# Cosine-similarity attention on one core: one score chunk of pair 24 exponentiated on VectorE, a shorter ring of cast V, a longer ring of exponentials, and new orders of work

## The chip, the core and the metric

The kernel runs on one core of one Trainium2 chip. The five engines that the profile names are TensorE (PE, with its weight loads as PEld), VectorE (DVE), ScalarE (ACT), GpSimd (POOL) and SyncE (SP), which here only issues transfers. The metric is the device time of the kernel in microseconds (us). Three runs of the kernel before gave 191.53, 191.48 and 190.59 us; the median is 191.48 us.

## The reference

Q, K and V have 8 batches of 12 heads, each 512 by 64, in float32, and tau is 0.1.

```python
Q_norm = Q / (np.linalg.norm(Q, axis=-1, keepdims=True) + 1e-10)
K_norm = K / (np.linalg.norm(K, axis=-1, keepdims=True) + 1e-10)
scores = np.einsum('bhqd,bhkd->bhqk', Q_norm, K_norm) / tau
weights = np.exp(scores - np.max(scores, axis=-1, keepdims=True))
weights = weights / (np.sum(weights, axis=-1, keepdims=True) + 1e-10)
return np.einsum('bhqk,bhkd->bhqd', weights, V)
```

Because the rows are normalised, a score lies between -10 and 10, and the kernel leaves the subtraction of the maximum out: a common factor of a row falls out when the row is divided by its sum.

## The kernel before, in words

The 96 heads are worked on as 48 pairs. All steps of a pair `s` are named, and a table (`ORDER`) lists, for each engine by itself, in which order that engine runs them. Nothing else decides the order: every engine runs its list from front to back, and a step that needs a result of another engine waits for that engine's semaphore, with everything behind it on the same list.

The steps of a pair are these.

- `LD.s.0`, `LD.s.1`, `LV.s` (SP): load Q, K and V of the pair, 256 KB each. `ST.s` stores the result.
- `SQ.s` (POOL): squares of Q and K in bf16 (line 250). `SSQ.s` (PE): eight matmuls with the identity that fold the squares into partial sums (line 268). `RED.s` (DVE): the sums of squares (line 276).
- `NEW.g.0` to `NEW.g.7` (DVE): inverse square roots by Newton steps, for a group `g` of one or two pairs, in the bank `nps` of PSUM (lines 397 to 409). The first three pairs take a logarithm (`LN`) and an exponential (`EX`, line 286) on ACT instead.
- `SCL.s.0` (DVE) and `SCL.s.1` (mostly POOL): Q and K times their inverse norms, to bf16 (line 296).
- `TR.s` (PE): sixteen transposes into PSUM (line 498). `EVA.s` (DVE): the copy of these to SBUF, the tile `qt` (line 504).
- `SCO.s.c` for four chunks `c` (PE): two matmuls of 512 columns, the scores of 128 keys against 512 queries for both heads (line 526). There are two buffers of scores, so `SCO` of a chunk has to wait until `EXP` two chunks earlier has read its buffer.
- `EXP.s.c` (ACT): the exponential of 1024 scores a partition, to bf16 in the tile `et` (line 542).
- `PV.s.h.t` (PE): eight groups of four matmuls of 65 columns, the exponentials times V with a column of ones (line 570). V is cast to bf16 by `VC.s` (POOL, line 547) into the ring `vb`.
- `RCP.s` and `NRM.s` (DVE): one over the row sums, and the product that makes the output (lines 584 and 586).

The chunks of all pairs form one sequence. PE works some pairs ahead of the products: while the scores of pair `s` are made, the products of pair `s-2` run between them. Below, a *slot* is what PE does from one `SCO` to the next.

The program can already put a chunk on DVE (the function `split`, steps `SCD` on PE and `EXD` on DVE), but the table `SPLIT` that names the chunks is empty, so that this code is not run. `SCD` makes the scores on top of a constant ("level") in PSUM, so that the bits of the float are already a linear guess of the exponential's bf16 bits; four steps `EXD.0` to `EXD.3` correct the guess by a cubic and write the 16 bits into `et`.

Of the kernel before, what the change touches and what calls it, by code (L numbers as in the profile page):

```python
# [28 lines left out]
class Program:  # L29
# [95 lines left out]
def bass_cosine_similarity_attention_kernel(  # L125
# [16 lines left out]
    R_QK, R_V, R_SQ, R_QN, R_QT, R_ET, R_O = 18, 6, 6, 5, 5, 3, 8  # L142
# [8 lines left out]
    vb = sb("vb", [128, R_QK, NT, 2, DIM + 1], bf16)  # L151
# [11 lines left out]
    level = sb("level", [128, 128 + SEQ], bf16)  # L163
    wd = [sb(f"wd{i}", [128, SEQ], f32) for i in range(2)]
# [51 lines left out]
    def scored(s):  # L216

        if s < 0:
            return []
        last = [("SCO", s, NT - 1) if s else ("SCO", 0, 1, NT - 1)]  # L220
        return last + [("SCD", s, h) for h in range(2) if s in SPLIT]

# [204 lines left out]
    def pair(s):  # L427
# [24 lines left out]
        if 0 < s < LOGS:  # L452
# [9 lines left out]
            for w, dst in ((0, rq), (1, r)):  # L462
                exps(s, (w,), dst, xl[s][:, w], ("LN", s), gain, free)
            scaled(s, 0, "dve", rq, [("EX", s, 0), ("EX", s, 1)])
            for j in range(2) if s == 1 else ():
                scaled(1, 1, eng, r, [("EX", 1, w) for w in range(2)], (j,), slice(2 * j, 2 * j + 2))
            if s > 1:
                scaled(s, 1, eng, r, [("EX", s, w) for w in range(2)])
        elif s:
# [5 lines left out]
            else:  # L475
                free = [("EX", LOGS - 1, w) for w in range(2)]
# [39 lines left out]
        for c in range(NT) if s else ():  # L516
# [23 lines left out]
            else:  # L540
# [5 lines left out]
        P.add(("VC", s), "pool", [("LV", s), key("PV", s - R_QK, 1, NT - 1), "vone"],  # L546
              lambda e: e.tensor_scalar(  # L547
                  out=vb[:, iq, :, :, 0:DIM].rearrange("p c h d -> p h c d"),
# [5 lines left out]
        for c in range(NT) if s in CHUNKED else ():  # L554
            def pv(e, c=c):
                for h in range(2):
                    for t in range(NT):
                        last = e.matmul(  # L558
                            out=o_ps[:, h, 65 * t : 65 * t + 65],
                            lhsT=et[iet][:, c, h, 128 * t : 128 * t + 128], rhs=vb[:, iq, c, h, :],  # L560
# [3 lines left out]
            P.add(("PV", s, c), "pe", [("EXP", s, c), ("VC", s), ("PV", s, c - 1) if c else None], pv,  # L564
                  take=[] if c else ["o0", "o1"], until=("NRM", s))
        for h in range(2) if s not in CHUNKED else ():
            for t in range(NT):
                def pv(e, h=h, t=t):
                    for c in range(NT):
                        last = e.matmul(  # L570
                            out=o_ps[:, h, 65 * t : 65 * t + 65],
                            lhsT=et[iet][:, c, h, 128 * t : 128 * t + 128], rhs=vb[:, iq, c, h, :],
# [5 lines left out]
                      [("EXP", s, NT - 1) if s else ("EXP", 0, 1, 1), ("VC", s), before,  # L578
                       *([("EXD", s, h, 3)] if s in SPLIT else []),
# [13 lines left out]
    def split(s, c, ready, iqt, iet):  # L593

        for h in range(2):
            hs = slice(64 * h, 64 * h + 64)

            def scd(e, hs=hs):
# [259 lines left out]
```

## Time and profile before

| | |
|---|---|
| median of three runs | 191.48 us (190.59 to 191.53) |
| span of the profiled execution, first to last instruction | 189.4 us |
| mean granted TensorE clock | 0.996 |
| ACT busy | 181.7 us, 96% |
| PE busy, modelled | 174.1 us, 92% |
| POOL busy | 160.7 us, 85% |
| DVE busy | 148.1 us, 78% |
| DMA | 50.8 MB, mean 268 GB/s |

The profile gives the span of its execution and no other time of it. The median of the runs is 2.1 us above that span. That is what lies around the first and the last instruction, and the difference between executions. A row of the page's groups reads: line, engine, operation, output from inputs, shapes, count, then the busy time, the mean length of one in ns, and the idle time just before. A row of the timeline begins with the start and the length in us; rows of the same kind in a run are merged with their count. Instructions of one engine may overlap at their ends, so the length of one is longer than the step from one start to the next.

### The profile page before, as it was taken

To read this page: it belongs to the slowest core of one execution; us is meant where nothing else is said; L and a number is where in the kernel's file an instruction comes from. 1 tells how busy PE (TensorE), PEld (TensorE's weight loads), DVE (VectorE), ACT (ScalarE), POOL (GpSimd) and SP (SyncE) were. 2 spreads that over 40 slices of the span, in tenths; PEclk is the share of its full clock that TensorE was granted. 3 is DMA by queue.
4 is the path that set the end of the run, shared out by engine and by line. 5 is a ranking of instruction groups with operands and counts; after the bars stand their busy time and mean duration, and the time that the engine had idled before them with its cause. 6 is when DMAs were issued, how large, how long until landed. Compare 5 with 4: busy or idle time off the path is not lost.

```text
span 189.4 us, 7341 instructions
## 1 busy us (share of the span) xinstructions
PE 174.1 (92%) x3078; PEld 110.7 (58%) x3078; DVE 148.1 (78%) x453; ACT 181.7 (96%) x210; POOL 160.7 (85%) x147
## 2 busy tenths in 40 slices
PE   7989998999999998999999999989989999987893
PEld 5446664665665665666555666556656666654552
DVE  1999987879877886898876968969888787787624
ACT  5699999999999999999999999999999999999993
POOL 1799999999999999999999999999997599562500
PEclk9999999999999999999999999999999999999998
DMA  6999999999469999999999959899959500754435
GB/s 169 338 352 349 350 350 349 350 376 383 151 197 356 291 345 315 269 376 323 359 361 378 271 167 336 257 332 345 328 160 313 168 12 9 211 177 140 141 107 173
DMA packets 52448, 50.80 MB, mean 268 GB/s; under 512 B 3136, under 2 KB 52416, under 8 KB 52416
## 3 DMA queue, kind: packets, MB, share of 16 engines
q1 hardware_dynamic: 51984, 50.02, 82.3%
q8 instruction: 24, 0.39, 0.9%
q10 hardware_dynamic: 432, 0.33, 0.6%
q14 instruction: 8, 0.07, 0.1%
HBM read 37.75 MB, written 12.58 MB: 266 GB/s over the span
## 4 chain that ended last, share of the span: by engine, by line
ACT 82%; DVE 7%; PE 7%; DMA 1%; issue 1%
ACT et L542 80%; PE scps L526 2%; DMA qk<-in_Q_dram 1%; DVE qn L296 1%; PE bps L570 1%; DVE ob L586 1%; DVE qt L504 1%; ACT et L371 1%; PE bps L339 1%; PE bps L558 1%; DVE nps L276 1%; PE bps L268 1%; DVE ob L643 1%; PE bps L498 0%; DVE xs L324 0%
## 5 line engine op out<-in xcount | busy, mean ns | idle before, releaser
L542 ACT ACTIVATE et<-scps 128x1024 bf16<-128x1024 f32 x184 | 169.1, 1128 | 0.5 <-PE scps L526 0.4
L250 POOL TENSOR_TENSOR sq<-qk 128x1024 bf16<-128x1024 f32 (+2 forms) x48 | 87.9, 1848 | 5.1 <-DMA qk<-in_Q_dram 4.9
L526 PE MATMUL scps<-qt 64*128 64x512 bf16 x376 | 74.4, 385 | 8.4 <-ACT et L542 6.1
L570 PEld LDWEIGHTS bps<-vb,et 128*128 128x128 bf16 x1472 | 51.4, 98 | 24.1 <-issue 18.0
L570 PE MATMUL bps<-vb,et 128*128 128x65 bf16 x1472 | 65.1, 194 | 0.2
L296 POOL TENSOR_TENSOR qn<-qk,rk 128x512 bf16<-128x512 f32 x44 | 45.8, 1051 | 11.8 <-DVE rk L405 11.7
L504 DVE COPY qt<-bps 128x1024 bf16<-128x1024 bf16 x46 | 31.8, 691 | 10.1 <-PE bps L498 9.4
L296 DVE TENSOR_TENSOR qn<-qk,nps 128x512 bf16<-128x512 f32 (+1 forms) x51 | 33.9, 671 | 0.8 <-ACT nps L286 0.2
L586 DVE TENSOR_TENSOR ob<-bps,rd 128x512 f32<-128x512 f32 x47 | 32.5, 691 | 1.2
L526 PEld LDWEIGHTS scps<-qt 64*128 64x128 bf16 x376 | 18.2, 93 | 25.3 <-ACT et L542 13.4
L547 POOL TENSOR_SCALAR vb<-vf 128x512 bf16<-128x512 f32 x48 | 29.9, 634 | 0.0
L268 PE MATMUL bps<-sq,ident 128*128 128x128 bf16 x376 | 29.1, 220 | 0.0
L268 PEld LDWEIGHTS bps<-sq,ident 128*128 128x128 bf16 x376 | 21.2, 98 | 9.4 <-issue 6.3
L584 DVE RECIPROCAL rd<-bps 128x8 f32<-128x8 f32 x47 | 9.7, 207 | 17.7 <-PE bps L570 14.3
L498 PE MATMUL bps<-ident,qn 64*128 64x64 bf16 x736 | 18.8, 191 | 2.4 <-DVE ob L586 0.4
L498 PEld LDWEIGHTS bps<-ident,qn 64*128 64x128 bf16 x736 | 14.2, 95 | 9.8 <-DVE nps L276 4.0
L276 DVE TENSOR_REDUCE nps<-bps 128x16 f32<-128x128 f32 x45 | 13.4, 297 | 1.8 <-PE bps L268 1.8
L397 DVE TENSOR_TENSOR nps<-nps,ys 128x32 f32<-128x32 f32 (+1 forms) x48 | 9.2, 193 | 0.9
L401 DVE SCALAR_TENSOR_TENSOR nps<-nps,ys 128x32 f32<-128x32 f32 (+1 forms) x48 | 9.1, 191 | 0.8
L237 PE MATMUL scps<-warm_in 128*128 128x256 bf16 x22 | 4.8, 402 | 1.1 <-DVE warm_in L232 1.1
L409 DVE TENSOR_SCALAR ys<-nps 128x32 int32<-128x32 int32 (+1 forms) x24 | 4.4, 183 | 0.5
L405 DVE SCALAR_TENSOR_TENSOR nps<-nps,ys 128x16 f32<-128x16 f32 (+1 forms) x25 | 4.3, 175 | 0.3
(44 smaller groups left out, 47.4 us busy)
## 6 DMA issues: line engine op xcount, KB each, us to landing
vf<-in_V_dram SPq DMA_DIRECT2D x48, 256.0 KB, 5.4
qk<-in_Q_dram SPq DMA_DIRECT2D x47, 256.0 KB, 5.9
qk<-in_K_dram SPq DMA_DIRECT2D x47, 256.0 KB, 5.7
out_dram<-ob SPq DMA_DIRECT2D x47, 256.0 KB, 4.4
qk<-in_Q_dram SPq DMA_DIRECT2D x2, 128.0 KB, 2.7
qk<-in_K_dram ACTq DMA_DIRECT2D x2, 128.0 KB, 2.9
out_dram<-ob SPq DMA_DIRECT2D x1, 128.0 KB, 2.2
out_dram<-ob SPq DMA_DIRECT2D x1, 64.0 KB, 1.9
```

The lines of the kernel that those rows point to most:

```text
L250: emit = lambda e: e.tensor_tensor(out=b, in0=a, in1=a, op=ALU.mult)
L268: last = e.matmul(out=ps[:, 0:128], lhsT=ident[:, :], rhs=sq[s % R_SQ][:, :, 8 * k : 8 * k + 8], start=(k == 0), stop=(k == 7))
L276: lambda e: e.tensor_reduce(out=dst(None), in_=ps[:, 0:128].rearrange("p (w g e) -> p w g e", w=2, e=8), axis=AX.X, op=ALU.add))
L296: lambda e: e.tensor_tensor(out=o, in0=x, in1=r, op=ALU.mult))
L498: last = e.transpose(t_ps[:, k, b, :], qn[s % R_QN][ks, b // NT, b % NT].rearrange("p h d -> p (h d)"), ident[ks, ks])
L504: lambda e, lo=lo, hi=hi: e.tensor_copy(out=qt[iqt][:, :].rearrange("p w t (k x) -> p k (w t) x", k=2)[:, :, lo:hi], in_=t_ps[:, :, lo:hi]))
L526: last = e.matmul(out=sc_ps[:, 2 * b + k, :], lhsT=qt[iqt][64 * h : 64 * h + 64, 1, n, :], rhs=qt[iqt][64 * h : 64 * h + 64, 0, :, :], sta ...
L542: lambda e, c=c, b=b: e.activation(out=et[iet][:, c, :, :], in_=sc_ps[:, 2 * b : 2 * b + 2, :], func=ACT.Exp, scale=scale, bias=bias))
L547: lambda e: e.tensor_scalar(out=vb[:, iq, :, :, 0:DIM].rearrange("p c h d -> p h c d"), in0=vf[iv][:, :, :].rearrange("p h (c d) -> p h c ...
L570: last = e.matmul(out=o_ps[:, h, 65 * t : 65 * t + 65], lhsT=et[iet][:, c, h, 128 * t : 128 * t + 128], rhs=vb[:, iq, c, h, :], start=(c = ...
L584: lambda e: e.reciprocal(out=rd[io][:, :], in_=grid[:, :, :, DIM]))
L586: lambda e: e.tensor_tensor(out=ob[io][:, :], in0=grid[:, :, :, 0:DIM], in1=rd[io][:, :].unsqueeze(3).to_broadcast([128, 2, NT, DIM]), op= ...
```

## The change

Six things are edited.

1. `SPLIT = {24: 1}`: chunk 1 of pair 24 leaves ACT and PE's sequence of scores (`EXP.24.1` and `SCO.24.1` are gone). DVE makes its exponentials. The three other chunks of pair 24 get a constant bias so that both ways have the same scale; the factor falls out with the row sum.
2. `split` is rewritten: the chunk is cut into four parts (head `h`, half `j` of the queries) of 256 columns, and their scores go to the upper half of the bank `nps` instead of a bank of their own. Each part has one `SCD` on PE (two matmuls of 256 columns) and four `EXD` on DVE. A part's `SCD` waits for the last step of the part before, and, by the new lines in `schedule`, for the last step on DVE's list before its first `EXD` that touches the bank `nps` (a `RED`, `NEW`, `SCL` or `EXD`), since PE writes into that bank.
3. The ring of exponentials `et` has four buffers instead of three (`R_ET`), so that `EXP.s` waits for the products of pair `s-4` instead of `s-3`. The ring of cast V, until now as long as that of Q and K (18), has nine (`R_VB`), so `VC.s` waits for the products of pair `s-9`.
4. `SCL.12.1` and `SCL.18.1` go from POOL to DVE, each with one short `NEW` step more.
5. In the first pairs, where DVE scales both Q and K, the two `EX` of 8 columns on ACT become one of 16 (pairs 1 and 2).
6. The lists of all engines are written anew. SP's too: but for two loads that trade places the first 32 transfers keep their sequence, later some loads and stores trade places.

```diff
+        last = None
+        for o in order["dve"]:
+            if o.key[0] == "EXD" and o.key[-1] == 0:
+                self.ops[("SCD", *o.key[1:-1])].needs.append(last)
+            if o.key[0] in ("RED", "NEW", "SCL", "EXD"):
+                last = o.key
...
-    R_QK, R_V, R_SQ, R_QN, R_QT, R_ET, R_O = 18, 6, 6, 5, 5, 3, 8
+    R_QK, R_V, R_SQ, R_QN, R_QT, R_ET, R_O, R_VB = 18, 6, 6, 5, 5, 4, 8, 9
...
-    y_u = x_ps[:, :].bitcast(u16).rearrange("p (x two) -> p x two", two=2)[:, :, 0]
+    y_ps = n_ps[:, 256:512]
+    y_u = y_ps.bitcast(u16).rearrange("p (x two) -> p x two", two=2)[:, :, 0]
...
-            for w, dst in ((0, rq), (1, r)):
-                exps(s, (w,), dst, xl[s][:, w], ("LN", s), gain, free)
+            both = eng == "dve"
+            for w, dst in ((0, spare[:, 16 * s - 8 : 16 * s + 8]),) if both else ((0, rq), (1, r)):
+                exps(s, (w,), dst, xl[s][:, :, :].rearrange("p w x -> p (w x)") if both else xl[s][:, w], ("LN", s), gain, free)
...
-        P.add(("VC", s), "pool", [("LV", s), key("PV", s - R_QK, 1, NT - 1), "vone"],
+        P.add(("VC", s), "pool", [("LV", s), key("PV", s - R_VB, 1, NT - 1), "vone"],
...
+            for j in range(2):
+                hs, qs = slice(64 * h, 64 * h + 64), slice(256 * j, 256 * j + 256)
+                def scd(e, hs=hs, j=j):
+                    e.matmul(out=y_ps, lhsT=level[hs, 0:128], rhs=level[hs, 128:384], start=True, stop=False)
+                    return e.matmul(
+                        out=y_ps, lhsT=qt[iqt][hs, 1, c, :], rhs=qt[iqt][hs, 0, 2 * j : 2 * j + 2, :], start=False, stop=True)
+                P.add(("SCD", s, h, j), "pe", ready + ["level"] + exd[-1:], scd)
+                w = wd[len(exd) % 2][:, :]
+                steps = [
+                    lambda e, w=w: e.tensor_scalar(
+                        out=w, in0=y_u, scalar1=1.0, scalar2=-65536.0, op0=ALU.mult, op1=ALU.add),
+                    lambda e, w=w: e.tensor_tensor(out=w, in0=y_u, in1=w, op=ALU.mult),
+                    lambda e, w=w: e.scalar_tensor_tensor(
+                        out=w, in0=y_u, scalar=65536.0 * CUBIC[1], in1=w, op0=ALU.add, op1=ALU.mult),
+                    lambda e, w=w, h=h, qs=qs: e.scalar_tensor_tensor(
+                        out=et[iet][:, c, h, qs].bitcast(u16), in0=w, scalar=128 * CUBIC[0] / 65536.0**3, in1=y_ps,
+                        op0=ALU.mult, op1=ALU.add)]
...
-ON = {'SQ.0.0.1': 'pool', 'SCL.2.1': 'dve', 'SCL.3.1': 'dve', 'LD.1.1': 'sp', 'SCL.1.1': 'dve'}
-SPLIT = {}
+ON = {'SQ.0.0.1': 'pool', 'SCL.2.1': 'dve', 'SCL.3.1': 'dve', 'LD.1.1': 'sp', 'SCL.1.1': 'dve', 'SCL.12.1': 'dve', 'SCL.18.1': 'dve'}
+SPLIT = {24: 1}
...
-        PV.22.0.0 PV.22.0.1 TR.25 SCO.24.1 PV.22.0.2 PV.22.0.3 SCO.24.2 PV.22.1.0 PV.22.1.1 PV.22.1.2 PV.22.1.3
+        SCO.24.0 PV.22.0.1 PV.22.0.2 PV.22.0.3 SCD.24.1.0 SCO.24.2 SSQ.29 SCO.24.3 PV.22.1.0 PV.22.1.1 PV.22.1.2
```

What the new lists do is seen at three places. The first is PE's list at the scores of pair 24. In these rows `scps<-qt` is an `SCO` (two matmuls a chunk), `bps<-vb,et` are products (four matmuls a group), `bps<-ident,qn` is a `TR`, `bps<-sq,ident` an `SSQ`, `nps<-level` with `nps<-qt` an `SCD`. Before, from `TR.25` to `SSQ.29`:

```order
L498 MATMUL bps<-ident,qn 128x64 x16
L526 MATMUL scps<-qt 128x512 x2
L570 MATMUL bps<-vb,et 128x65 x8
L526 MATMUL scps<-qt 128x512 x2
L570 MATMUL bps<-vb,et 128x65 x16
L526 MATMUL scps<-qt 128x512 x2
L268 MATMUL bps<-sq,ident 128x128 x8
```

With the change, from `SCD.24.0.1` to `SSQ.29`:

```order
L610 MATMUL nps<-level 128x256
L611 MATMUL nps<-qt 128x256
L535 MATMUL scps<-qt 128x512 x2
L580 MATMUL bps<-vb,et 128x65 x4
L507 MATMUL bps<-ident,qn 128x64 x16
L535 MATMUL scps<-qt 128x512 x2
L580 MATMUL bps<-vb,et 128x65 x12
L610 MATMUL nps<-level 128x256
L611 MATMUL nps<-qt 128x256
L535 MATMUL scps<-qt 128x512 x2
L275 MATMUL bps<-sq,ident 128x128 x8
```

One `SCO` is gone (24.1), and two `SCD` stand directly ahead of `SCO.23.3` and `SCO.24.2`. The second place is DVE's list at the same time. Here `rd<-bps` is an `RCP`, `ob<-bps` an `NRM`, `nps<-bps` a `RED`, `qt<-bps` an `EVA`, `wd<-nps` and `et<-wd,nps` are `EXD`, the short ones with `ys` are `NEW`. Before, from `EVA.24` to `EVA.25`:

```order
L504 COPY qt<-bps 128x2x8x64
L401 SCALAR_TENSOR_TENSOR nps<-nps,ys 128x32
L584 RECIPROCAL rd<-bps 128x8
L586 TENSOR_TENSOR ob<-bps,rd 128x512
L276 TENSOR_REDUCE nps<-bps 128x2x8
L405 SCALAR_TENSOR_TENSOR ys<-nps,ys 128x32
L397 TENSOR_TENSOR nps<-nps,ys 128x32
L401 SCALAR_TENSOR_TENSOR nps<-nps,ys 128x32
L405 SCALAR_TENSOR_TENSOR nps<-nps,ys 128x16
L405 SCALAR_TENSOR_TENSOR rk<-nps,ys 128x16
L504 COPY qt<-bps 128x2x8x64
```

With the change, from the end of part 0 to `EVA.25` (the seven rows ahead of these are `EVA.24`, the first three `EXD` of part 0, two `NEW` and `RCP.21`):

```order
L622 SCALAR_TENSOR_TENSOR et<-wd,nps 128x256
L596 TENSOR_TENSOR ob<-bps,rd 128x512
L617 TENSOR_SCALAR wd<-nps 128x256
L283 TENSOR_REDUCE nps<-bps 128x2x8
L619 TENSOR_TENSOR wd<-nps,wd 128x256
L408 SCALAR_TENSOR_TENSOR nps<-nps,ys 128x32
L620 SCALAR_TENSOR_TENSOR wd<-nps,wd 128x256
L412 SCALAR_TENSOR_TENSOR nps<-nps,ys 128x16
L622 SCALAR_TENSOR_TENSOR et<-wd,nps 128x256
L513 COPY qt<-bps 128x2x8x64
```

Eight `EXD` now stand between the two `EVA`, and the other eight between `EVA.25` and `EVA.27`, always with another step between two of them but for the last pair. The third place is PE's list at the scores of pair 20. Before, from `SCO.20.1` to `SCO.20.3`:

```order
L526 MATMUL scps<-qt 128x512 x2
L498 MATMUL bps<-ident,qn 128x64 x16
L570 MATMUL bps<-vb,et 128x65 x8
L526 MATMUL scps<-qt 128x512 x2
L570 MATMUL bps<-vb,et 128x65 x16
L526 MATMUL scps<-qt 128x512 x2
```

With the change, from `SCO.20.1` to `TR.22`; the row of four is `SCO.20.2` and `SCO.20.3`:

```order
L535 MATMUL scps<-qt 128x512 x2
L580 MATMUL bps<-vb,et 128x65 x16
L275 MATMUL bps<-sq,ident 128x128 x8
L535 MATMUL scps<-qt 128x512 x4
L507 MATMUL bps<-ident,qn 128x64 x16
```

The slot of `SCO.20.1` now holds four groups of products and an `SSQ`; before, an `SSQ` behind four groups stood in the slots of `SCO.3.0` and `SCO.40.2` alone.

More of the change, by code (lines that the diff above doesn't have):

```diff
@@ L220, in scored @@
         last = [("SCO", s, NT - 1) if s else ("SCO", 0, 1, NT - 1)]
-        return last + [("SCD", s, h) for h in range(2) if s in SPLIT]
+        return last + [("SCD", s, h, j) for h in range(2) for j in range(2) if s in SPLIT]
     P.add("one", "pool", [], lambda e: e.memset(ones[:, :], 1.0))
@@ L595, in split @@
         for h in range(2):
-            hs = slice(64 * h, 64 * h + 64)
-            def scd(e, hs=hs):
-                e.matmul(out=x_ps[:, :], lhsT=level[hs, 0:128], rhs=level[hs, 128 : 128 + SEQ], start=True, stop=False)
-                return e.matmul(out=x_ps[:, :], lhsT=qt[iqt][hs, 1, c, :], rhs=qt[iqt][hs, 0, :, :], start=False, stop=True)
-            P.add(("SCD", s, h), "pe", ready + ["level"], scd, take=["x"], until=("EXD", s, h, 3))
-            w, done = wd[len(exd) % 2], exd[-2:-1]
```

328 lines of the change are left out of this document (165 added, 163 removed).

## The prediction

> **What bounds the kernel now.** I read the page first: the busy lines and the chain that ended last.
>
> ```profile
> span 189.4 us, 7341 instructions
> PE 174.1 (92%) x3078; PEld 110.7 (58%) x3078; DVE 148.1 (78%) x453; ACT 181.7 (96%) x210; POOL 160.7 (85%) x147
> ACT 82%; DVE 7%; PE 7%; DMA 1%; issue 1%
> ```
>
> ACT is busy for 96% of the span and is 82% of the chain. The chain in order of time shows where it is never left:
>
> ```profile
> 29.06 130.32 ACT et L542 x142
> 159.38 0.02 issue
> 159.41 22.11 ACT et L542 x24
> ```
>
> From 29.06 us to 181.52 us the chain is exponentials alone. A removed chunk is therefore worth the step from one to the next, not the length of one, since two overlap at their ends. Two rows of ACT's timeline give the step where nothing is late: eleven chunks begin at 65.64, and the eleventh begins at 74.69.
>
> ```profile
> 65.64 10.30 ACT L542 ACTIVATE et<-scps 128x1024 bf16<-128x1024 f32 x11
> 74.69 2.17 ACT L542 ACTIVATE et<-scps 128x1024 bf16<-128x1024 f32 x2
> ```
>
> That is 9.05 us for ten steps, 0.905 us each. From 29.06 to 159.41 the chain makes 142 steps in 130.35 us; at 0.905 they would take 128.5, so 1.8 us are lost there although ACT hardly looks idle. Two places show to whom, in PE's and ACT's timelines:
>
> ```profile
> 157.61 0.39 PE L526 MATMUL scps<-qt 64*128 64x512 bf16 x2
> 157.93 0.67 PE L570 MATMUL bps<-vb,et 128*128 128x65 bf16 x16
> 158.43 0.61 PE L268 MATMUL bps<-sq,ident 128*128 128x128 bf16 x8
> 158.98 0.85 PE L526 MATMUL scps<-qt 64*128 64x512 bf16 x4
> 158.09 3.25 ACT L542 ACTIVATE et<-scps 128x1024 bf16<-128x1024 f32 x3
> 117.24 0.39 PE L526 MATMUL scps<-qt 64*128 64x512 bf16 x2 [0.29 <-ACT et L542]
> 117.56 0.91 PE L570 MATMUL bps<-vb,et 128*128 128x65 bf16 x24
> 118.41 0.39 PE L526 MATMUL scps<-qt 64*128 64x512 bf16 x2
> 117.78 1.24 ACT L542 ACTIVATE et<-scps 128x1024 bf16<-128x1024 f32 x1
> 118.84 1.10 ACT L542 ACTIVATE et<-scps 128x1024 bf16<-128x1024 f32 x1
> ```
>
> In the first, PE has scores, four groups of products (0.50 us to the next start) and an `SSQ` (0.55) in one slot: 1.37 us from `SCO` to `SCO`. The exponential that needs the later scores starts at 159.41, 1.32 us after the one at 158.09, so 0.41 late. In the second a slot has six groups, 1.17 us, and the exponential is 1.06 after the one before: 0.15 late. So ACT is the bound, PE's list decides how late its work comes, and a slot over about 1 us costs.
>
> **The change part by part.** *The removed chunk* takes one step off ACT: 0.905 us. The ends of this are 0 (if PE, not ACT, then sets the pace) and 0.92 (130.35 us over 142, lateness shared); I take 0.905 because PE waits for ACT before many scores, as at 117.24.
>
> *The head.* Each of the two merges of `EX` can take at most the second row's step.
>
> ```profile
> 8.98 1.19 PE L366 MATMUL scps<-qt 64*128 64x512 bf16 x4
> 9.32 0.28 ACT L286 ACTIVATE nps<-xl 128x8 f32<-128x8 f32 x2
> 9.62 1.94 ACT L371 ACTIVATE et<-scps 128x1024 bf16<-128x1024 f32 x2
> 11.69 0.28 ACT L286 ACTIVATE nps<-xl 128x8 f32<-128x8 f32 x2
> 11.91 1.00 ACT L371 ACTIVATE et<-scps 128x1024 bf16<-128x1024 f32 x1
> L286 ACT ACTIVATE nps<-xl 128x8 f32<-128x8 f32 x5 | 0.7, 173 | 0.1
> ```
>
> At 9.62 the exponential has to wait for the scores that PE makes from 8.98 on, so the first merge gives nothing. The second stands between two exponentials; two `EX` take 0.28 there and one 0.17: 0.11 us gained, with 0 and 0.14 as ends.
>
> *The added work on DVE* is sixteen `EXD` of 256 columns from PSUM. None ran before. The nearest rows are products of the same width:
>
> ```profile
> L333 DVE TENSOR_TENSOR qn<-qk,bps 128x256 bf16<-128x256 f32 x2 | 0.8, 418 | 0.0
> 5.17 0.75 DVE L333 TENSOR_TENSOR qn<-qk,bps 128x256 bf16<-128x256 f32 x2
> 98.03 0.18 DVE L405 SCALAR_TENSOR_TENSOR nps<-nps,ys 128x16 f32<-128x16 f32 x1
> 98.12 0.16 DVE L405 SCALAR_TENSOR_TENSOR rk<-nps,ys 128x16 f32<-128x16 f32 x1
> 98.20 0.68 DVE L504 COPY qt<-bps 128x1024 bf16<-128x1024 bf16 x1
> 98.80 0.68 DVE L296 TENSOR_TENSOR qn<-qk,nps 128x512 bf16<-128x512 f32 x1
> ```
>
> One takes 0.42 us; two that do not need each other take 0.75, so the second costs 0.33. The same overlap stands at 98.03 to 98.80: steps of 0.09, 0.08 and 0.60 where the lengths are 0.18, 0.16 and 0.68. Sixteen `EXD` cost 5.3 us of DVE if each lies beside independent work, and 16 x 0.44 = 7.0 if each waits for the one before (0.42 and 0.02 to start). Does this fit? From `EVA.24` to `EVA.28` the new list has 4 `EVA`, 4 `NRM`, 4 `SCL`, 4 `RCP`, 3 `RED`, 13 `NEW`. At 0.60 for the twelve large ones, 0.15 for `RCP`, 0.22 for `RED`, 0.12 for `NEW`, the overlapped steps, that is 7.2 + 0.6 + 0.7 + 1.6 = 10.1 us, and 15.4 with the `EXD`. `TR.24` and `TR.28` lie eighteen score slots apart on the new list: 18 x 0.905 = 16.3 us. It fits with 0.9 us to spare.
>
> *The waits.* Each `SCD` stands on PE's list until DVE has done the `EXD` of the part before, and the next `SCO` stands behind it. I follow the tightest, `SCD.24.1.0` with `SCO.24.2` behind it, from the start of `EXP.22.2` as zero, with a slot's buffer free 1.13 us after the start of the exponential two chunks earlier (the mean length):
>
> ```profile
> L542 ACT ACTIVATE et<-scps 128x1024 bf16<-128x1024 f32 x184 | 169.1, 1128 | 0.5 <-PE scps L526 0.4
> 1.10 4.24 PE L237 MATMUL scps<-warm_in 128*128 128x256 bf16 x19 [1.10 <-DVE warm_in L232]
> ```
>
> `SCO.22.1` can go at -1.59, `SSQ.27` follows at -1.27 and its `RED` ends at about -0.36, so `TR.24` starts at about -0.2 and `EVA.24` runs from 0.2 to 0.9. `SCD.24.0.0` follows. It has two matmuls of 256 columns; in the warm-up, nineteen take 4.24 us, some 0.21 each, and a pair of 512 columns takes 0.32 to the next start (117.24 to 117.56), so I bound it by 0.2 and 0.43 and take 0.32. Four `EXD` at 0.44 end at 3.1, then `NRM.21` at 3.7. `SCD.24.0.1` is done at 3.75 too, since it stands behind `SCO.23.2`. The second part's four, with `RED.28` between, end at 5.6. `SCD.24.1.0` goes, `SCO.24.2` starts at 6.0 and ends at 6.4, and `EXP.24.2` was due at 6.33: 0.1 late. I take 0.2 us for the four parts together. The ends are 0, and 0.9 if each `EXD` of two parts takes 0.1 longer.
>
> On PE the four `SCD` add 1.3 us and `SCO.24.1` leaves with 0.32; the net 1.0 lies in slots that PE waits in. Without that cover it is the 0.4 of a late slot.
>
> *The rest of PE's list.* Between `EXP.5.1` and `EXP.40.3` the old list has five slots of six groups, ten of five and one of four with `SSQ`. The new one has four, five and one of these, and one of three groups with `SSQ` (`SCO.33.2`). Priced as above: old 5 x 0.15 + 0.41, and the remaining 0.64 of the 1.8 for the ten and all else; new 4 x 0.15 + 0.41, my estimate of 0.35 for the slot with a group less, and half of the 0.64, 1.7 together. The gain is 0.1 us. The ends are a gain of 0.9 (half of the old lateness goes) and a loss of 0.9 (the two slots with `SSQ` and the ones with `SCD` cost 0.4 each, and what they push costs again).
>
> *POOL, transfers, rings.*
>
> ```profile
> 30.00:141.00 111.00, 110.53 (x97) 1.00 0.96 308
> L296 POOL TENSOR_TENSOR qn<-qk,rk 128x512 bf16<-128x512 f32 x44 | 45.8, 1051 | 11.8 <-DVE rk L405 11.7
> POOL sq L250 <- DMA qk<-in_Q_dram: 4.9, 2, 3.6
> ```
>
> POOL has no idle time from 30 to 141 us (110.53 of 111), and two `SCL` of 1.05 us leave it: 2.1 us earlier for all behind. DVE takes them for 0.60 each beside its idle fifth. That is worth nothing on the path while POOL is not late, and covers the faster ACT. POOL waits for loads only in the head (twice, 3.6 us at most), so the traded transfers and the shorter ring of V cost nothing while loads come ahead; one load behind a store that waits would cost up to those 3.6 us. The fourth buffer of `et` only loosens a wait.
>
> **Sum.** -0.905 - 0.11 + 0.2 - 0.1 = -0.9 us on the span of 189.4, so 188.5, and 191.48 - 0.9 = 190.6 on the median.
>
> **The rivals.** *The waits eat it:* four new slots (`SCO.20.1`, `SCO.33.2`, `SCO.22.3`, `SCO.24.0`) each cost about what the slot at 157.61 cost, +0.9 beyond my sum. The slots' length speaks for it; that slots with `SSQ` alone cost nothing speaks against. 191.5 us.
>
> *DVE runs out of time at the split*, the one that ends slower. If its instructions do not overlap, the window from `EVA.24` to `EVA.28` costs the full lengths: twelve at 0.69, four `RCP` at 0.21, three `RED` at 0.30, thirteen `NEW` at 0.18, sixteen `EXD` at 0.44, 8.3 + 0.8 + 0.9 + 2.3 + 7.0 = 19.3 against 16.3. `EVA.28` and the scores behind it come 3.0 us late: 193.6. It decides from a lateness of 2 us on. The rows from 98.03 on speak against it.
>
> ```profile
> L586 DVE TENSOR_TENSOR ob<-bps,rd 128x512 f32<-128x512 f32 x47 | 32.5, 691 | 1.2
> L276 DVE TENSOR_REDUCE nps<-bps 128x16 f32<-128x128 f32 x45 | 13.4, 297 | 1.8 <-PE bps L268 1.8
> L584 DVE RECIPROCAL rd<-bps 128x8 f32<-128x8 f32 x47 | 9.7, 207 | 17.7 <-PE bps L570 14.3
> ```
>
> [...]
>
> *The new list is simply better:* POOL's 2.1 us and the fourth buffer let PE come in time, and half of the old 1.8 us of lateness goes too. 189.7 us.
>
> **How the numbers follow.** My forecast (190.1 to 191.1) has 0.50, the waits 0.25, the better list 0.15, DVE out of time 0.10. About 0.5%, 0.96 us, is what a measurement of this kernel can tell from no change. Of my forecast 0.26 lies beyond that and 0.24 within; the better list is all faster; the waits are within for 0.18 and slower for 0.07. Faster 0.41, same 0.42, slower 0.17. For the range I leave out the end of the better list and most of DVE out of time: 189.4 to 192.0.
>
> **What would show it.** One run of exponentials, 183 in line 542's successor, at 0.905 a step outside late slots; an `EXD` at 0.42 us in length; PE's wait before `SCO.24.2` under 0.5 us; the last exponential 0.9 us earlier. I am wrong if ACT shows a gap of over 0.5 us between `EXP.22.2` and `EXP.28.0`, if an `EXD` takes over 0.55, if the slots at `SCO.20.1` or `SCO.33.2` cost over 0.6 each, or if POOL waits for a load after 30 us.

## The result: slower by 1.6%

| | before | changed |
|---|---|---|
| median | 191.09 us (190.59 to 191.53, 4 runs) | 194.03 us (193.72 to 194.47, 4 runs) |
| span of the profiled execution | 189.4 us | 192.3 us |
| predicted median | | 190.6 us (189.4 to 192.0) |

The ratio is 1.0156, with a 95% interval of 1.0129 to 1.0184. The prediction had the wrong sign, and the time lies outside its range. Of 85 further executions of the kernel before, 17 had a mean granted clock of 0.982 to 0.991 and took 192.98 to 194.54 us, while all four executions of the changed kernel had such a clock (0.988 to 0.991).

These are the lines of the changed kernel's page that answer to the ones shown of before (span, busy time, the clock that the throttle granted in 40 slices, the chain of waits, the exponentials).

```profile
span 192.3 us, 7371 instructions
PE 176.6 (92%) x3084; PEld 111.6 (58%) x3084; DVE 154.3 (80%) x475; ACT 182.1 (95%) x207; POOL 158.0 (82%) x145
PEclk9999997999999999999999999999999999999998
ACT 74%; PE 13%; DVE 8%; issue 2%; DMA 2%; ACTq 0%; DVEq 0%
L551 ACT ACTIVATE et<-scps 128x1024 bf16<-128x1024 f32 x183 | 169.8, 1059 | 3.0 <-PE scps L535 2.7
```

The reader is to see three things. ACT's share of the chain fell from 82% to 74%. ACT now waits 2.7 us for scores, where the row of before had 0.4. And one slice of the granted clock reads 7, where before has nines up to the last slice, which reads 8 in both.

**Where the time went.** Each exponential has the same name in both kernels, so the start of each in one trace minus its start in the other (times from the span's start) says where the difference grows:

| stretch | changed minus before grows by, us |
|---|---|
| up to `EXP.1.0` (the head, with the merged `EX`) | -0.15 |
| at `EXP.3.2` | +0.39 |
| from there to `EXP.5.0` | -0.02 |
| at `EXP.5.1` | +1.18 |
| from there to `EXP.7.3` | +1.57 |
| from there to `EXP.24.0` | +0.45 |
| at `EXP.24.2` (one chunk fewer) | -0.86 |
| from there to `EXP.47.2` | +0.50 |
| sum | +3.06 |

The span grows by 2.9 us, since what follows the last exponential is 0.15 us shorter. The removed chunk gave what was forecast. Its neighbourhood did too, as the rows of the tile `wd` show (the four kinds of `EXD`: shortest, median and longest in ns; and who waited for them), and ACT's timeline across the split, which is one unbroken run:

```profile
L617 DVE TENSOR_SCALAR wd<-nps x4: 415/415/425, 97.1 to 105.0; 128x256 f32<-128x256 uint16 x4
L622 DVE SCALAR_TENSOR_TENSOR et<-wd,nps x4: 410/420/420, 98.5 to 108.7; 128x256 uint16<-128x256 f32 x4
  PEld nps L610: 0.3, 2
91.06 25.13 ACT L551 ACTIVATE et<-scps 128x1024 bf16<-128x1024 f32 x27
```

So the loss is elsewhere: 2.7 us between 28 and 41 us, from `EXP.5.1` to `EXP.7.3`, and another 1 us spread over the rest. The chain of waits passes through the first place:

```profile
28.27 0.32 PE scps L535
28.59 1.45 issue
30.04 0.39 PE scps L535
30.42 0.55 PE bps L275 x8
30.98 0.54 PE scps L535 x2
...
33.94 0.52 PE scps L535 x2
34.48 1.03 ACT et L551
```

"issue" is time in which PE waited for nothing that the profile shows: no semaphore, no operand. It stands between the two matmuls of `SCO.5.1`, and the second of them is a plain matmul on the tile `qt` that `SCO.5.0` had read from 27.28 us on. Behind it the pair of score matmuls takes 0.54 where the first took 0.32 to the next start. The table by stretches (PE, PEld, DVE, ACT, POOL busy, then the granted clock, the share of the DMA engines, GB/s) shows why:

```profile
28.00:30.00 2.00, 0.59 (x10) 0.24 (x6) 0.90 (x2) 0.94 (x2) 2.00 (x5) 1.00 1.08 343
30.00:32.00 2.00, 1.96 (x27) 1.13 (x28) 0.89 (x4) 1.47 (x2) 0.94 (x1) 0.71 1.11 349
32.00:34.00 2.00, 2.00 (x27) 1.34 (x24) 1.46 (x7) 1.37 (x2) 0.35 (x1) 0.50 1.10 348
34.00:36.00 2.00, 1.62 (x18) 0.62 (x17) 1.02 (x3) 1.75 (x3) 2.00 (x2) 0.93 1.12 352
```

After the gap the clock stands at one half: the shares missing to 1.00, each times 2 us, are 0.58, 1.00 and 0.14 us, 1.72 us of lost clock together, that is 3.4 us at one half. Four more of the traces below have one such fall amid the work (`LD.16.0` back, no split, held at 4, and the split on the old lists with the hold), and it lasts 3.4 us in each.

The +0.39 at `EXP.3.2` is a smaller gap of the same kind, in the weight loads of an `SSQ`:

```profile
21.48 0.39 PEld L275 LDWEIGHTS bps<-sq,ident 128*128 128x128 bf16 x7 [0.38 <-issue]
```

The kernel before has the long gap at the same instruction, only shorter, and no fall of the clock:

```profile
28.64 0.39 PE L526 MATMUL scps<-qt 64*128 64x512 bf16 x1 [0.32 <-issue]
28.00:30.00 2.00, 1.61 (x15) 0.69 (x16) 1.40 (x5) 1.63 (x3) 2.00 (x3) 1.00 1.11 351
```

### The profile page after: what moved, and what is told of

Same layout as the page of the kernel before. It is cut to its first block, busy times and chain, and to the rows that moved or that the text cites. A ratio compares the mean times of both kernels' runs of the same rounds, so it can differ in the third digit from the quotient of the medians.

```text
span 192.3 us, 7371 instructions
## 1 busy us (share of the span) xinstructions
PE 176.6 (92%) x3084; PEld 111.6 (58%) x3084; DVE 154.3 (80%) x475; ACT 182.1 (95%) x207; POOL 158.0 (82%) x145
## 4 chain that ended last, share of the span: by engine, by line
ACT 74%; PE 13%; DVE 8%; issue 2%; DMA 2%; ACTq 0%; DVEq 0%
ACT et L551 72%; PE scps L535 4%; PE bps L580 3%; DVE qn L303 2%; DMA qk<-in_K_dram 2%; PE bps L507 1%; DVE ob L596 1%; DVE qt L513 1%; PE bps L275 1%; ACT et L378 1%; PE bps L346 1%; DVE nps L283 1%; PE bps L567 1%; PE scps L373 1%; DVE ob L655 1%
## 5 line engine op out<-in xcount | busy, mean ns | idle before, releaser
L580 PE MATMUL bps<-vb,et 128*128 128x65 bf16 x1472 | 67.2, 195 | 0.3 <-DVE qt L513 0.2
L580 PEld LDWEIGHTS bps<-vb,et 128*128 128x128 bf16 x1472 | 52.3, 98 | 25.3 <-issue 16.0
L303 POOL TENSOR_TENSOR qn<-qk,rk 128x512 bf16<-128x512 f32 x42 | 43.5, 1045 | 8.0 <-DVE rk L412 7.6
L303 DVE TENSOR_TENSOR qn<-qk,nps 128x512 bf16<-128x512 f32 (+1 forms) x53 | 34.8, 669 | 0.5 <-ACT nps L293 0.3
L412 DVE SCALAR_TENSOR_TENSOR ys<-nps,ys 128x32 f32<-128x32 f32 (+1 forms) x24 | 4.4, 184 | 0.4
```

What stands on the lines that cost most here:

```text
L303: lambda e: e.tensor_tensor(out=o, in0=x, in1=r, op=ALU.mult))
L580: last = e.matmul(out=o_ps[:, h, 65 * t : 65 * t + 65], lhsT=et[iet][:, c, h, 128 * t : 128 * t + 128], rhs=vb[:, s % R_VB, c, h, :], star ...
```

## Three theories

**Fetch.** In both kernels PE has executed exactly 690 instructions (matmuls and weight loads) when the gap begins. The page's DMA part has a queue of the kind "instruction"; for the changed kernel it reads, and in the stretch from 27.4 to 28.8 us of its trace:

```profile
q8 instruction: 24, 0.39, 0.9%
q8 instruction: 1, 0.02, 5.2%
```

The page doesn't say whose instructions these are; that they are PE's is my reading. If all 24 packets (0.39 MB, so 16 KB each) are, they hold 257 of the 6168 PE instructions each, an estimate from these counts. One packet takes 1.16 us (5.2% of 16 engines times 1.4 us), and none lies between 20 and 27.4 us. The smaller gap at 21 us begins after 438 instructions, 252 fewer than 690, and ends 1.5 us after the packet before that one (18.8 to 20.0 us). The theory: PE runs out of instructions because this packet stands in the DMA engines with the loads, which there take

```profile
vf<-in_V_dram SPq DMA_DIRECT2D x8, 256.0 KB, 7.8
```

7.8 us from issue to landing (the median from 10 to 30 us, 7.3 for Q and K, with 9 or 10 of them on their way), and the gap lets the clock fall. The kernel before has as many on their way, and lands them in 7.0 to 7.3 us. **Order.** The new lists of PE and DVE make the scores of pair 5 late. **Split.** DVE's added work costs the time. What decides between them: the first predicts that fewer loads in flight remove the gap with all lists unchanged.

## Fewer loads in flight

Two kernels let each of SP's transfers number 8 to 59 also wait for the landing of the one four places earlier. No engine's order is touched.

```diff
+        sp = order["sp"]
+        for i in range(8, 60):
+            j = i - 4
+            while any(sp[k].slot == sp[j].slot for k in range(j + 1, i)):
+                j -= 1
+            sp[i].needs.append(sp[j].key)
         for e, ops in order.items():
             before = {}
```

The hold on the changed kernel:

> The changed kernel, in which each of SP's transfers number 8 to 59 also waits until the transfer four places earlier (or, where that one shares its semaphore with a later one, the one before it) has landed, so that about four loads are in flight instead of six or more. The order of every engine is as in the changed kernel. Fetch theory (PE's own instructions come late at 28 us because their packet stands behind the loads, and the clock then falls): PE's gap at SCO.5.1 is under 0.5 us, no granted clock of 0.5 behind it, 190.3 to 191.3 us. Order theory (the new lists of PE and DVE make the scores of pair 5 late): the same gap and 194.0 us, give or take 0.5. Split theory (DVE's work at the split costs the 3 us): 194.0 as well.

And on the kernel before:

> The same hold on the kernel before. Fetch theory: its own gap of 0.7 us at the same instruction of PE goes as well, 0.5 us less, 190.6. Order theory: 191.1, no change. Either is wrong if the hold starves the head: then POOL waits for loads and the time is above 191.6.

Measured: 199.07 us (197.27 to 199.55) and 197.99 us (197.04 to 198.34), both slower. As times these are misses. The traces answer the question all the same. PE's timeline of the held changed kernel at the place of the gap, and a load's time to landing from 10 to 30 us:

```profile
28.89 0.39 PE L541 MATMUL scps<-qt 64*128 64x512 bf16 x2
vf<-in_V_dram SPq DMA_DIRECT2D x6, 256.0 KB, 4.3
```

The two matmuls of `SCO.5.1` are one row again: the gap is gone, in both kernels, and `EXP.5.1` is 0.52 us nearer to its predecessor than in the kernel before. In the changed kernel the packet came at 23.2 us instead of 27.5. In the kernel before it came at 26.0, hardly earlier than the 26.25 without the hold, but PE reached the place 0.6 us later. Four in flight don't keep the DMA engines full (mean 271 GB/s from 10 to 30 us in the held changed kernel, where the changed kernel has 349), and ACT falls behind in many places (the changed kernel at 21 to 23 us and from 37 us on, the kernel before from 43 us on): the last exponential comes 7.3 and 5.7 us later than in the kernel before without the hold.

By accident the pair also says something on the clock. Both starve PE near 50 us. First the kernel before with the hold, then the changed one, PE's gap and the stretch behind it:

```profile
50.08 0.62 PE L274 MATMUL bps<-sq,ident 128*128 128x128 bf16 x8 [1.86 <-POOL sq L256]
50.00:52.00 2.00, 1.92 (x32) 1.36 (x33) 1.23 (x5) 0.69 (x1) 2.00 (x3) 1.00 0.94 294
```
```profile
51.47 0.93 PE L281 MATMUL bps<-sq,ident 128*128 128x128 bf16 x8 [1.73 <-POOL sq L263]
52.00:54.00 2.00, 2.00 (x20) 1.02 (x18) 0.51 (x3) 1.01 (x1) 1.26 (x1) 0.50 0.87 244
```

Behind a gap of 1.86 us the clock reads 1.00, behind one of 1.73 us 0.50. So the length of a gap alone doesn't decide.

## One load fewer, and no split

In the changed kernel one load of 256 KB, `LD.16.0`, is issued nine places earlier than before. This kernel moves it back:

```diff
-  ... LV.8 LD.16.0 LD.12.1 LD.14.0 ... LV.10 LV.7 LD.15.0 ...
+  ... LV.8 LD.12.1 LD.14.0 ... LV.10 LV.7 LD.16.0 LD.15.0 ...
```

> The changed kernel with one transfer, LD.16.0, moved nine places back in SP's list, behind LV.7, where the kernel before has it: one load of 256 KB fewer is on its way from about 20 us on. Fetch theory, if this load is what makes the fetch later than before: the packet of 27.37 us comes 0.7 to 1 us earlier, PE's gap is about the 0.7 us of the kernel before, 191.0 us. Fetch theory, if the lateness has another source (the head that is 0.3 us earlier): 193 to 194. Order theory: 194.0.

Measured: 194.12 us (192.7 to 194.56). The gap is unchanged, so the load isn't what makes the packet later:

```profile
30.21 0.39 PE L535 MATMUL scps<-qt 64*128 64x512 bf16 x1 [1.50 <-issue]
```

The other kernel takes the split out and leaves everything else:

```diff
-SPLIT = {24: 1}
+SPLIT = {}
```

with `SCO.24.1` and `EXP.24.1` on the lists ahead of `SCO.24.2` and `EXP.24.2`, and without `SCD`, `EXD` and the two `level` steps.

> The changed kernel without the split: the four SCD, sixteen EXD and the level are left out, SCO.24.1 and EXP.24.1 stand on the lists again ahead of SCO.24.2 and EXP.24.2; all else as in the changed kernel. Fetch theory and order theory: the head is as late as in the changed kernel and ACT has one step of 0.905 us more, 194.9 us. Split theory: 191 to 192 us, since what costs is gone.

Measured: 194.84 us (194.5 to 197.64), gap and clock as in the changed kernel (1.52 us of idle PE, a granted clock of 0.50 from 32 to 34 us). The split theory falls.

## A milder hold, and a count that moves

Six loads in flight instead of four, and only for the transfers 8 to 35 (`range(8, 36)` and `i - 6` in the code above), on the changed kernel, on the kernel before, and on the changed kernel without the split:

> The changed kernel with a milder hold: SP's transfers number 8 to 35 wait for the landing of the one six places earlier, so that about six loads are on their way instead of nine or ten, and everything after them is free. Fetch theory: the packet with PE's instructions that came at 27.5 us comes by 25.5, PE's gap at SCO.5.1 is under 0.4 us, there is no granted clock of 0.5, and 189.8 to 191.0 us are left. If six loads in flight still starve the head as four did, EXP.3.2 is more than 0.3 us later than in the changed kernel and the time is 191 to 193. Order theory: 194.

> The same hold on the kernel before. Fetch theory: its own gap of 0.7 us goes, 190.6 to 191.2 us, and the ratio to the held changed kernel is then what the change itself is worth, 0.7 to 1.0 us. Order theory: 191.2.

> The held changed kernel without the split (no SCD, no EXD, the chunk 24.1 on ACT again). All theories that leave the split its gain: 0.9 us above the held changed kernel. If the split costs as much as it saves: no difference.

| | median | against the kernel before, 95% |
|---|---|---|
| changed, held | 190.70 us (190.55 to 192.08) | 0.9962 (0.9926 to 0.9998) |
| before, held | 190.57 us (190.24 to 191.4) | 0.9946 (0.9910 to 0.9982) |
| changed, held, no split | 193.95 us (191.63 to 195.44) | too far apart to use |

The changed kernel gains 3.3 us by the hold, inside the range that the fetch theory gave, and it is now faster than the kernel before. PE's timeline at the place of the gap, the clock, and a load's time to landing:

```profile
27.59 0.39 PE L541 MATMUL scps<-qt 64*128 64x512 bf16 x2
27.91 0.62 PE L281 MATMUL bps<-sq,ident 128*128 128x128 bf16 x8
PEclk9999999999999999999999999999999999999999
qk<-in_Q_dram SPq DMA_DIRECT2D x11, 256.0 KB, 4.8
```

No gap, no fall of the clock, and the packet at 24.3 us. Six in flight are enough to feed the head (352 GB/s at 26 to 28 us; 329 from 10 to 30 us, against 349). The kernel before gains 0.9 us by the same hold. In the traces 0.52 us of this is its short gap, at `EXP.5.1`, and 0.24 us a first exponential that starts earlier. That start varies between executions (7.7 to 8.9 us in the four kernels with the changed head and the hold of six), so a better scale of the traces is the time from the start of the first exponential to the end of the last: 178.6 us in the kernel before, 181.6 in the changed one, 178.1 in both held kernels. Between the two held kernels 0.7 to 1.0 us were expected, and there is no difference; the section on the lists takes this up.

Second, the count. This kernel puts 38 more PE instructions ahead of everything:

```diff
-WARM = 19
+WARM = 38
-            out=bank[:, 0:256], lhsT=warm_in[:, 0:128], rhs=warm_in[:, :], start=True, stop=True))
+            out=bank[0:32, 0:128], lhsT=warm_in[:, 0:32], rhs=warm_in[:, 0:128], start=True, stop=True))
```

(the second edit for the warm-up only).

> The changed kernel with 38 warm-up matmuls of 128 columns from 32 columns of weights instead of 19 of 256 from 128: about the same time for the warm-up, but 38 more PE instructions (a weight load and a matmul each) ahead of everything. All lists are otherwise unchanged. Fetch theory: the place at which PE runs out of instructions is a count, so the gap of over 1 us stands 38 instructions earlier in the program, ahead of SCO.5.0 (count 652 of the changed kernel) and no longer inside SCO.5.1 (count 690); 193 to 195 us. Order theory: the gap stays inside SCO.5.1, which the lists make late.

Measured: 190.78 us (190.42 to 191.98), ratio 0.9975 (0.9941 to 1.001). The gap neither stayed nor moved: it vanished, because the packet came at 24.2 us although nine loads were in flight. That is a miss for my form of the fetch theory, which had the packet's delay fixed by the loads, and a second blow to the order theory: the lists are those of the changed kernel, and 3.2 us are gone. From the first exponential to the last it takes 178.1 us, as the held changed kernel.

Over the traces of all kernels but the one of 237 us (below) one regularity holds. Where PE waits for "issue" ahead of a matmul for more than 0.15 us, it does so at its instruction 690, in two traces at 438 or 1194 too (252 fewer and 504 more), and the wait ends 1.2 to 1.6 us after the end of a packet. Where the packet had ended 1.5 us or more before PE got to instruction 690, there is no gap; where it had ended 1.0 us before that or later, there is one. The shortest lead without a gap is that of the kernel before held at 4 (packet from 26.0 to 27.0 us, instruction at 28.5); the five kernels with the hold of six that the table leaves out have no gap and leads of 1.75 to 3.0 us.

| trace | packet starts, us | gap from start to start at 690, us |
|---|---|---|
| changed, held at 4 | 23.2 | 0 |
| 38 warm-up matmuls | 24.2 | 0.2 (0.1 of it a wait for DVE) |
| changed, held at 6 | 24.3 | 0 |
| split on the old lists, free (below) | 25.5 | 0.4 |
| before with the new head (below) | 26.1 | 0.7 |
| before | 26.25 | 0.7 |
| changed with the old head (below) | 26.3 | 1.0 |
| changed without the split | 27.0 | 1.9 |
| changed | 27.5 | 1.8 |
| changed, `LD.16.0` back | 27.7 | 1.9 |

## What the held kernels still owe: the lists

Held, the changed kernel is no faster than the held kernel before (190.70 and 190.57), although its split gives 0.85 us there too. Something takes that back. To measure it, the held kernel without the split ran again:

> The held changed kernel without the split once more, since its first times lay far apart (191.6 to 195.4): the changed lists and the merged EX on as many exponentials as the held kernel before has. List theory: the changed lists lose 1.1 to 1.2 us against those of before, the merged EX gain 0.3, so 0.8 to 0.9 above both held kernels, 191.5 us. If the lists lose nothing: 190.3, and the split then gives nothing.

Measured: 191.95 us (191.43 to 193.71, 12 runs), ratio 1.0031 (1.0001 to 1.0062). Its first exponential came 1.5 us later than the other's, since the first large loads landed later (on its chain of waits a load of K takes 5.90 us, to 8.06, on the other's one takes 3.08, to 4.30), so the trace is the better scale. The chains of waits (start, length, then ACT's exponentials with their count) of the held kernel before and of this one have the same 174 exponentials at their end:

```profile
20.94 137.66 ACT et L548 x150
158.62 22.11 ACT et L548 x24
```
```profile
22.16 16.71 ACT et L557 x18
38.87 40.61 ACT et L557 x44
79.49 6.52 ACT et L557 x7
86.03 82.16 ACT et L557 x89
168.21 14.83 ACT et L557 x16
```

From 20.94 to 180.73 are 159.79 us; from 22.16 to 183.04 are 160.88. With nothing removed, the new lists (with the rings and the two moved `SCL`) lose 1.09 us against the old ones. Where they do is seen in PE's timeline of the held changed kernel, with the split, at `SCO.27.1`:

```profile
107.86 0.39 PE L541 MATMUL scps<-qt 64*128 64x512 bf16 x2
108.44 0.41 PE L513 MATMUL bps<-ident,qn 64*128 64x64 bf16 x16 [0.19 <-DVE nps L289]
108.78 0.54 PE L586 MATMUL bps<-vb,et 128*128 128x65 bf16 x12
109.25 0.39 PE L541 MATMUL scps<-qt 64*128 64x512 bf16 x2
109.58 0.29 PE L586 MATMUL bps<-vb,et 128*128 128x65 bf16 x4
109.73 0.61 PE L281 MATMUL bps<-sq,ident 128*128 128x128 bf16 x8
110.27 0.39 PE L541 MATMUL scps<-qt 64*128 64x512 bf16 x2
```

A slot with a `TR` and three groups of products takes 1.39 us, 0.19 of it a wait for DVE, and the next, one group and an `SSQ`, 1.02. The exponentials 27.2 and 27.3 are 0.26 and 0.11 late. Without the split the slot takes 1.23 us and 27.2 is 0.14 late, so 0.12 us here belong to the split. The same pattern costs 0.28 at 30.2 and 30.3 and 0.21 at 39.1 and 39.2; a slot of six groups ahead of one with two groups and an `SSQ` costs 0.32 at 18.2 and 18.3, and four groups with an `SSQ` (`SCO.20.1`) 0.20. The kernel before has late slots as well (0.41 at `EXP.40.3`), only fewer: from `EXP.5.1` to `EXP.43.3` nine exponentials of the held one start 0.08 us or more later than a step of 0.905 allows, 1.5 us together, and 21 of the held one with the new lists and no split, 2.7 us together.

Two attempts to get this back failed. The first puts the split and the merged `EX` on the lists of before, with the new lists of PE and DVE (and in this stretch POOL's too) only from `SCO.19.0` to `SCO.31.0`, once held and once free:

> The split and the merged EX on the lists of the kernel before: the changed kernel's code, with the changed lists of PE and DVE only from SCO.19.0 to SCO.31.0 (the stretch with the split), those of the kernel before everywhere else; SCL.12.1 and SCL.18.1 on POOL, three buffers of exponentials and eighteen of cast V as before; the hold of six. List theory (with the late instructions out of the way, the changed lists lose about 1.2 us outside the split, which is why the held changed kernel is no faster than the held kernel before): 0.7 to 1.0 us below both held kernels, 189.6 to 190.0. If the lists lose nothing and the split itself gives nothing on the whole: 190.6, as the held kernels.

> The kernel with the split on the lists of the kernel before, without the hold. Fetch theory: PE's gap inside SCO.5.1 is back at 0.5 us or more; 0.5 us above the held one if the clock stays, about 3 us above it if the gap is long enough for a granted clock of 0.5, so 190.2 or 192.7. If the gap belongs to the changed head lists alone: as the held one.

Measured: 196.0 us (195.22 to 197.58) and 196.69 us (195.04 to 199.18). The step of the split is there (-0.86 in the held one), and from `EXP.0.1.1` to `EXP.18.3`, on the old lists, only 0.1 us is lost against the held kernel before, where the held changed kernel loses 0.6. But around the seams of the lists, at `EXP.19.1`, `EXP.20.2` and `EXP.29.2`, ACT waits for scores (the held one):

```profile
80.89 4.83 ACT L557 ACTIVATE et<-scps 128x1024 bf16<-128x1024 f32 x5 [1.12 <-PE scps L541]
86.55 18.44 ACT L557 ACTIVATE et<-scps 128x1024 bf16<-128x1024 f32 x20 [0.83 <-PE scps L541]
121.84 2.12 ACT L557 ACTIVATE et<-scps 128x1024 bf16<-128x1024 f32 x2 [2.16 <-PE scps L541]
```

Ahead of the last of these PE waits 2.00 us for POOL, and the granted clock is 0.50 from 122 to 124 us. So this says what the split is worth, and not what a whole kernel with it would take. In the free one the gap at 690 was 0.4 us, a little under the 0.5 expected.

The second attempt reordered the lists of PE, DVE and POOL by a replay of the measured durations:

> The held changed kernel with the lists of PE, DVE and POOL between pair 4 and pair 45 reordered (nothing added or left out), so that by a replay of the measured durations the late exponentials of the held changed kernel (those at 12.2, 18.2, 18.3, 20.2, 27.2 and others) come in time. List theory: most of the 1.2 us that the changed lists lose comes back, 189.3 to 190.0 us, below both held kernels. If lateness of single score slots isn't what the lists lose: 190.7, as the held changed kernel, or more, where the new order has late places of its own.

Measured: 237.02 us (236.3 to 238.07). The chain of waits, which had been ACT's, is

```profile
POOL 37%; PE 26%; issue 12%; ACT 10%; DVE 7%; DMA 5%; SPq 2%; POOLq 0%
```

The replay took the times at which loads land as given, while POOL's new order decides when buffers come free for SP. That this is what failed is argued from the chain and not shown by a run. That late slots can be taken away by reordering therefore stays open.

The fourth buffer of exponentials was undone alone, on the held changed kernel (`R_ET` 3):

> The held changed kernel with three buffers of exponentials instead of four. If the fourth buffer only loosens a wait that does not come last: 190.7, no change from the held changed kernel. If the changed lists need it: some exponentials wait for products of three pairs earlier, and the time is above 191.3.

Measured: 191.02 us (190.36 to 192.82) against 190.70 held: no difference that can be told, as expected. The traces agree: 178.1 us from the first exponential to the last in both.

## What stays open: why the packet is later

The last pair swaps the lists of PE, DVE and POOL in the head (up to `SCO.5.2`, `EVA.9`, `VC.4`) between the two kernels, without a hold.

> The changed kernel, without any hold, with the lists of PE (up to SCO.5.2), DVE (up to EVA.9) and POOL (up to VC.4) in the order of the kernel before; behind these places the changed lists. Head-list theory (the new order in the head makes the packet with PE's instructions come later): the gap at SCO.5.1 is 0.7 us or less as in the kernel before, no granted clock of 0.5, 191.2 us. If it isn't the order (but the 0.3 us by which the merged EX bring the head forward, or where the loads stand): the gap of over 1 us and the clock of 0.5 stay, 194.0 us.

> The reverse: the kernel before with the changed order of PE, DVE and POOL in the head, up to the same places. Head-list theory: a gap of over 1 us at SCO.5.1, a granted clock of 0.5 behind it, 193.5 to 194.5 us. If it isn't the order: 191.4 us, as the kernel before.

Measured: 193.13 us (192.88 to 195.52) and 192.94 us (191.58 to 194.27). PE at the gap, the changed kernel with the old head and then the kernel before with the new one:

```profile
28.86 0.39 PE L535 MATMUL scps<-qt 64*128 64x512 bf16 x1 [0.59 <-issue]
```
```profile
28.66 0.39 PE L526 MATMUL scps<-qt 64*128 64x512 bf16 x1 [0.28 <-issue]
```

The old head made the gap shorter (0.59 of idle PE instead of 1.45) and kept the clock, which is what the head-list theory said; 1.3 us of its time are lost at the seam, at `EXP.7.1`. But the new head on the kernel before did not make this gap longer, which it had to. It brought two smaller ones that the kernel before does not have: 0.24 us in the weight loads ahead of `EXP.3.2`, where the changed kernel has one too, and 0.33 us at instruction 1194, at 44 us. Its ten executions range over 2.7 us, with mean granted clocks from 0.982 to 1.0, and the trace is that of the second fastest (191.77 us), so it doesn't show whether the long gap has become more frequent. The order in the head seems to be a part of it, and not the whole. What fixes the moment at which a packet of instructions is served among the loads isn't settled.

## Why the prediction was wrong, by its steps

- **The removed chunk**, -0.905: right, 0.81 to 0.86 at its place in every kernel with the split.
- **The merged `EX`**, -0.11, with nothing for the first merge: right as far as can be told. The second merge gave 0.09 in this trace. Between `EXP.0.0.0` and `EXP.0.0.2`, where the first stands, this trace gains 0.13 and those of the other kernels with the changed code 0.2 to 0.3, but the kernel before with the new head, which has no merge, gains 0.21 there too, and the two kernels with the split on the old lists, which have it, gain nothing. No run isolates the merge.
- **`EXD` and the waits at the split**, 0.42 us an instruction and 0.2 us of waits: right. An `EXD` takes 0.410 to 0.425, and 0.45 from start to start where the one that needs it follows directly (108.24 to 108.69 us). PE waits 0.3 us for two of them, ACT runs through. Two exponentials are 0.12 late by the split, `EXP.24.3` and (in the held kernels) `EXP.27.2`, about the 0.2 that was priced. The rival in which DVE runs out of time is refuted, since it needed a gap of 2 us there.
- **The rest of PE's list**, -0.1 with ends of -0.9 and +0.9: wrong, +1.09. I counted kinds of slots over the whole list and priced them singly. What stands at the late places is a full slot followed by another one, and a `TR` with three or four groups (1.23 us without a wait), which my count left out because it looked at groups and `SSQ` alone: the new list has eleven slots of this second kind between `EXP.5.1` and `EXP.40.3`, the old one four. This is read from the traces, and no run isolates it. The rest of the list is the term that was mis-sized, and it alone turns the forecast of a gain of 0.9 into no gain.
- **What lies ahead of 29.06 us**: the step that failed worst. The prediction looked for lateness only in the unbroken run of exponentials that begins there, and put it down to PE's list. The hold takes nothing from these 1.8 us (from `EXP.5.1` to `EXP.40.3` 130.38 us with it and 130.35 without). The prediction didn't ask why the run begins where it does. In the chain of before, these two rows stand ahead of 29.06:

```profile
28.32 0.32 issue
28.64 0.40 PE scps L526
```

`EXP.5.1` is 0.52 us late there, because PE goes on late without waiting for any result. In the view of waits of before, "PE scps" with its wait for "issue" of 0.3 us is the only matmul that waits for "issue", and I read over it. So the mechanism that decided the result, a PE whose instructions come late (as I read the gap) and then a clock of one half, was put at nothing and was no rival at all. It accounts for the +0.39 at `EXP.3.2`, which the hold of six removes, the +1.18 at `EXP.5.1` and about 1.2 of the +1.57 behind it: 2.8 of the 3.06 us.

- **POOL, transfers, rings at nothing**: right for what I listed. POOL waits for no load after 30 us, the fourth buffer makes no difference, nor does the moved load. But I asked only who waits for the loads' data, not what else uses the DMA engines.

Of the signs that I had named as "wrong if", none appeared. The tripwires stood where I had looked: at the split, at the new slots and at POOL. Only the last exponential, 3.1 us later instead of 0.9 earlier, gave it away.

## What to carry to other kernels

A wait for "issue" on a single ordinary matmul, where the others of its line have none, is worth an explanation before a change is priced: it may be the instructions themselves that are late, above all if it stands at the same count of instructions in two kernels. In this kernel, with a DMA share of 1.06 or more from 24 to 36 us, six loads in flight instead of nine or ten gave 0.9 us to the kernel before and 3.3 us to the changed one. But 38 more PE instructions ahead of everything, with nine loads in flight, gave the changed kernel as much, so it isn't shown that the number of loads is what helped. And a list that was written anew is to be priced by its runs of full slots in sequence, on both sides of the change, since the gain of one chunk, 0.905 us, is lost by four late places like the ones above (0.28, 0.21, 0.32 and 0.20 us).

## Unexpected in the hardware

- In this kernel PE stood idle in the middle of its list, waiting for nothing that the profile shows: with nine or ten loads of 256 KB in flight for 0.32 us in the kernel before and for 1.45 us in the changed one, both times with 690 instructions executed. The page has 24 packets of 16 KB in a queue "instruction", whose time counts on the same 16 DMA engines as the data (0.9% beside 80.0%). That the gaps are late instructions is read from their places, 252 instructions apart or twice that, and from the packet that ends 1.2 to 1.6 us ahead of each restart. Where the packet had ended 1.5 us or more before PE got to instruction 690, there is no gap.
- Behind the gap of 1.45 us of PE the clock stood at one half for 3.4 us, and some 1.2 us more were lost there (the 1.57 us from `EXP.5.1` to `EXP.7.3`, less the 0.33 that the held changed kernel loses there with a full clock). Behind a gap of 1.86 us in the kernel before, held at 4, the clock read 1.00.
